# One gathered tile's query: four weight buffers, scores kept in row buffers and searched block by block, steps emitted three at a time

## The chip, the cores and the metric

The kernel runs on one core of a Trainium2 chip. The metric is the time of one execution on the device in microseconds (us), smaller is better. PE is the matrix engine, DVE the vector engine, ACT the scalar engine, POOL the GpSimd engine; SP issues transfers. Each engine works through its own instructions in the order in which they stand.

## What is computed

One layer of a decoder for 1024 prompt tokens and 64 sample tokens: an input projection, two token mixers (retention and a recurrent one), an output projection, then a mixture of experts with product keys, then a gated embedding. The part that matters here is the expert layer:

```python
q = (xb @ wq).reshape(PEER_BLOCK, PEER_HEADS, 2, PEER_DKEY // 2)
s = jnp.einsum('phcd,hcnd->phcn', q, keys)          # 8 heads x 2 halves, 128 keys each
sv, si = lax.top_k(s, 16)
cand = sv[:, :, 0, :, None] + sv[:, :, 1, None, :]
cv, ci = lax.top_k(cand.reshape(...), 16)
e = take(si[:, :, 0], ci // 16) * 128 + take(si[:, :, 1], ci % 16)
gsm = softmax(cv)
hval = einsum('pd,phkd->phk', xb, u_tab[e])         # 128 rows of u_tab per token
y = einsum('phk,phkd->pd', gelu(hval) * gsm, v_tab[e])
```

## The kernel before

The 1088 tokens are nine tiles: 0 to 7 of 128 tokens, tile 8 of 64. Tiles 4 to 7 (`G2`) go through the experts densely: every expert is multiplied with every token and weighted. Tiles 0, 1, 8 (`E0`) and 2, 3 (`G1`) are **gathered**: for each of a token's 128 chosen experts, POOL issues one indirect transfer that brings a row of 1024 numbers for each of 128 tokens into a row buffer (`grow<-in_pu`, later `grow<-in_pv`, line 1144), and DVE multiplies or accumulates it (lines 1158 and 1172). That is 576 + 576 = 1152 transfers. `grow` runs through a ring of row buffers, so POOL issues as DVE frees them.

The program goes through these stages, read off the profile's time table: first projection and mixer (0 to 360 us); the projection of tiles 4 to 8 (`group_a` on `A2`, 360 to about 583 us: first the 40 steps of `a_ret`, with `pret` as the result and `rope`, `gsig`, `retd` behind it, then `a_rw` with `prw`, `rb`, `fdst`); the other mixers with the output rows of each tile (`group_b`, to about 1700); the last rows and the dense tiles' query (to 2060); the hidden layer of the dense tiles with their gates (to 2560); the second half of the dense experts in two parts (to 3577); and the end, `ple`, the gated embedding and final norm for tiles 0, 1, 8, 4 to 7, 2, 3 in this order.

The gathered work is written as one generator, `early`. It emits tile 0's query (`early_query`), then tile 0's gathers with the queries of tiles 1 and 8 threaded in, then the gathers of tiles 1 and 8. During the projection of `A2` each projection step is followed by `IE` steps of `early`; in the mixers by one each, up to 150. What is left comes after the dense query. The emitted order isn't the final one: the program is put through a list scheduler with a timeline model, which moves instructions along each engine, so an emitted place acts as a priority.

`early_query` takes a tile's normed rows (`exn`), turns them (`exT`), and for each of 16 blocks `hc` loads 512 KB of query weights (`ewq`) and 64 KB of keys (`ekT`), makes the query (`epq`, `eqT`) and its 128 scores (`es`). Before, the scores of two blocks are staged in a buffer with tag `sv` or `si` and stored to memory (`sd`); at the end two loads of eight blocks each bring them back, and `topk` searches them with `pick` (five DVE operations a block: two maxima of eight, two index searches, one replacement; lines 1043 to 1047). The tile's results are called `sv` and `si`, and take the buffers with those two tags. Then `topk` sums candidates (`ce`, with `sf` for the indices), searches the sums (`cv`, `ci`), finds the expert numbers with eight `eq` on POOL and eight `ef` on DVE, and writes `eid`; the gathers need `eid`.

Row buffers of the pool `early`, 4 KB a partition each: `V` twice, `W`, `xy`, `Wq` four times, `xT`. Tile 0's query takes its weights through the two `V`; the reloaded scores lie in `W` and a `Wq`. The gathers run through `V`, `V`, `W`, `xy`, and the tile's rows for the products (`gx`) come through `xy`.

Of the kernel before, what the change touches and what calls it, by code (L numbers as in the profile page):

```python
# [8 lines left out]
F32 = mybir.dt.float32  # L9
# [3 lines left out]
U32 = mybir.dt.uint32  # L13
# [168 lines left out]
E0 = [0, 1, 8]  # L182
# [8 lines left out]
IB = 2  # L191
PGT = "a"
SPL = "gv"
IE = 2
IA = 2
G2 = [4, 5, 6, 7]
RSTART = 2
# [2 lines left out]
QB = 4  # L200
# [17 lines left out]
class K:  # L218
# [431 lines left out]
    def first_mix(self, es):  # L650
# [3 lines left out]
        return self.mixers(self.cw, A0[0])  # L654

    def group_b(self, tiles, early):

        done = []
        self.b2 = 2
        with ExitStack() as e:  # L660
# [12 lines left out]
            for i, t in enumerate(tiles + [None]):  # L673
                cur, nxt = nxt, self.mixers(rp, t) if t is not None else None
                if i >= 2:
                    done.append(tiles[i - 2])
                live = nxt is not None
                while live or cur is not None:
                    if cur is not None:
                        if next(cur, "end") == "end":  # L680
                            cur = None
                    if i >= RSTART:
                        for _ in range(RRATE):
                            if next(rows, "end") == "end" and done:
                                rows = self.c_rows(self.co, done.pop(0))
                    if live:
                        live = next(nxt, "end") != "chain"
                    for _ in range(ERATE if E0[1] in self.rowed else 0):
                        if steps < EB:
                            steps += 1  # L690
                            next(early, None)
# [497 lines left out]
    def early_query(self, wp, t, wtag, wbufs, stags):  # L1189

        nc, I = self.nc, self.I
        n = SIZE[t]
        xn = wp.tile([128, D], F32, name="exn", tag=wtag, bufs=wbufs)
        nc.sync.dma_start(xn[:n], self.xd[t][:n])
        xT = wp.tile([128, 8, 128], F32, name="exT", tag="xT")
        for k in range(2):
            p = self.ps("etr", "a").rearrange("p (a b) -> p a b", a=4)
            for j in range(4):
                d = 4 * k + j
                nc.tensor.transpose(p[:, j, :n], xn[:n, d * 128:d * 128 + 128], self.c("ident")[:n, :n])  # L1200
            nc.scalar.activation(xT[:, 4 * k:4 * k + 4, :n], p[:, :, :n], AF.Copy)
            yield
        for hc in range(16):
            kT = wp.tile([128, 128], F32, name="ekT", tag=("cv", "ci")[hc % 2])
            nc.sync.dma_start(kT, I['keysT'][:, hc])
            w = wp.tile([128, 8, 128], F32, name="ewq", tag=wtag, bufs=wbufs)
            nc.sync.dma_start(w, I['wq'][hc])
            if hc % 2 == 0:
                st = wp.tile([128, 2, 128], F32, name="es", tag=("sv", "si")[hc // 2 % 2])
            p = self.ps("epq", "a")  # L1210
            for k in range(8):
                nc.tensor.matmul(p[:, :n], w[:, k], xT[:, k, :n], start=k == 0, stop=k == 7)
            qT = wp.tile([128, 128], F32, name="eqT", tag=("cf", "ef")[hc % 2])
            nc.scalar.activation(qT[:, :n], p[:, :n], AF.Copy)
            nc.tensor.matmul(p[:n, 128:256], qT[:, :n], kT, start=True, stop=True)
            nc.scalar.activation(st[:n, hc % 2], p[:n, 128:256], AF.Copy)
            if hc % 2:
                nc.scalar.dma_start(self.sd[t][:n, hc - 1:hc + 1], st[:n])
            yield
        s = []  # L1220
        for j in range(2):
            s.append(wp.tile([128, 8, 128], F32, name="es", tag=stags[j], bufs=QB if stags[j] == "Wq" else 1))
            nc.sync.dma_start(s[j][:n], self.sd[t][:n, 8 * j:8 * j + 8])
        yield
        ce = wp.tile([128, 2, 8, 50], F32, name="ce", tag="Wq", bufs=QB)
        yield from self.topk(wp, t, [s[j // 8][:, j % 8] for j in range(16)], dict(eq=dict(tag="xT")), (ce[:, 0], ce[:, 1]))

    def early(self, wp):

        rows = ("V", "V", "W", "xy")  # L1230
        yield from self.early_query(wp, E0[0], "V", 2, ("W", "Wq"))
        g = self.gather(wp, E0[0], rows, acc=self.acc)
        for t in E0[1:]:
            while t not in self.rowed:
                next(g, None)
                yield
            for _ in self.early_query(wp, t, "Wq", QB, ("Wq", "xT")):
                next(g, None)
                yield
        yield from g  # L1240
        for t in E0[1:]:
            yield from self.gather(wp, t, rows + ("xT",) * (t == E0[-1]), acc=self.acc)
# [201 lines left out]
    def build(self):  # L1444
# [3 lines left out]
        with self.es:  # L1448
# [28 lines left out]
            for _ in a:  # L1477
                for _ in range(IE):
                    next(early, None)
# [100 lines left out]
```

## Time and profile before

| | us |
|---|---|
| Median of 3 runs | 3758.44 |
| The three runs | 3747.60, 3758.44, 3776.36 |
| The profiled execution | 3747.65 |
| Its span, first to last instruction | 3745.9 |
| PE busy | 3294.1 |
| DVE busy | 2856.0 |
| POOL busy | 2336.2 |
| ACT busy | 1217.6 |

The profile is of one execution; what follows is read from it. A row of the timeline gives start, length, engine, line, operation, output and input, and in brackets how long the engine had been idle and for whom. A row of the table by stretch gives for each engine its busy time and number of instructions, then the granted PE clock (1.00 is full), the share of the transfer engines in use, and GB/s.

### The profile page before, as it was taken

The numbers are of one execution on the slowest core, as the hardware profiler recorded it, in microseconds if no ns is written. First come the engines' busy times: TensorE is split into PE (matmuls) and PEld (weight loads), VectorE is DVE, ScalarE is ACT, GpSimd is POOL, SyncE is SP. The second block draws the span as 40 slices with busy tenths as digits, with TensorE's granted clock in tenths as the row PEclk, the third lists the DMA queues.
The fourth block names the chain that finished last, engine by engine and source line by source line (L and its number), as shares of the span: only waits on it lengthen the run. The fifth ranks groups of instructions, "written<-read, shape, count | busy, mean of one in ns | idle before, by whom it ended". The sixth has DMA issues, their size and how long they took to land. (4 is left out here: it accounts for less than half of the span.)

```text
span 3745.9 us, 52394 instructions
## 1 busy us (share of the span) xinstructions
PE 3294.1 (88%) x17749; PEld 2742.5 (73%) x17749; DVE 2856.0 (76%) x5655; ACT 1217.6 (33%) x2260; POOL 2336.2 (62%) x2068
## 2 busy tenths in 40 slices
PE   7799995868869978884899999998999999989979
PEld 7698994644747866673787888887888877767757
DVE  4454388878797698886897998875777787888885
ACT  4232220111202111211222788793333333333322
POOL 5364176455364555554558877867888888888751
PEclk9799995667968566876999999999999999999989
DMA  7266578889778877888769888899999999999982
GB/s 254 81 216 212 187 244 289 276 286 311 258 249 313 311 268 253 285 273 320 254 216 317 298 311 320 332 340 334 337 347 342 328 354 371 374 370 368 339 279 89
DMA packets 425286, 1077.84 MB, mean 288 GB/s; under 512 B 46459, under 2 KB 144505, under 8 KB 420346
## 3 DMA queue, kind: packets, MB, share of 16 engines
q0 software_dynamic: 165888, 604.05, 45.5%
q1 hardware_dynamic: 203102, 378.60, 30.6%
q10 hardware_dynamic: 56028, 91.84, 6.6%
q8 instruction: 141, 2.31, 0.2%
q14 instruction: 127, 1.04, 0.1%
HBM read 982.51 MB, written 91.75 MB: 287 GB/s over the span
## 5 line engine op out<-in xcount | busy, mean ns | idle before, releaser
L1144 POOL DMA_INDIRECT grow<-in_pv,eid x576 | 567.4, 985 | 464.1 <-DVE gacc L1172 289.0
L1144 POOL DMA_INDIRECT grow<-in_pu,eid x576 | 558.1, 969 | 405.6 <-DVE grow L1158 228.0
L1172 DVE SCALAR_TENSOR_TENSOR gacc<-grow,ac,gacc 128x1024 f32<-128x1024 f32 x571 | 731.8, 1282 | 87.0 <-DMA grow<-in_pv,eid 80.3
L1158 DVE SCALAR_TENSOR_TENSOR grow<-grow,gacc 128x1024 f32<-128x1024 f32 x576 | 691.6, 1213 | 131.0 <-DMA grow<-in_pu,eid 124.1
L332 PE MATMUL ph<-cx,uh 128*128 128x512 f32 x1024 | 406.3, 397 | 17.5 <-DVE al L305 9.8
L1318 PE MATMUL py<-ah,vh 128*128 128x512 f32 x1024 | 403.3, 394 | 19.7 <-ACT vh L303 19.7
L333 PE MATMUL ph<-cx,uh 128*128 128x512 f32 x1024 | 404.9, 395 | 0.0
L1319 PE MATMUL py<-al,vh 128*128 128x512 f32 x1024 | 402.4, 393 | 2.6 <-DVE al L305 2.6
L307 POOL TENSOR_TENSOR vl<-vraw,vh 128x640 fp32r<-128x640 f32 (+1 forms) x224 | 326.2, 1460 | 34.9 <-ACT vh L303 17.5
L307 POOL TENSOR_TENSOR ul<-uraw,uh 128x1024 fp32r<-128x1024 f32 x128 | 307.7, 2404 | 64.5 <-issue 26.8
L1321 PE MATMUL py<-ah,vl 128*128 128x512 f32 x1024 | 275.9, 397 | 11.4 <-POOL vl L307 11.1
L335 PE MATMUL ph<-cx,ul 128*128 128x512 f32 x1024 | 263.2, 395 | 2.9 <-POOL ul L307 2.9
L303 ACT ACTIVATE vh<-vraw 128x640 fp32r<-128x640 f32 (+1 forms) x224 | 154.9, 692 | 301.8 <-DMA vraw<-in_pvd 105.6
L1318 PEld LDWEIGHTS py<-ah,vh 128*128 128x128 f32 x1024 | 193.5, 189 | 68.5 <-ACT vh L303 27.0
L332 PEld LDWEIGHTS ph<-cx,uh 128*128 128x128 f32 x1024 | 194.5, 190 | 58.0 <-DVE al L305 10.2
L1321 PEld LDWEIGHTS py<-ah,vl 128*128 128x128 f32 x1024 | 191.5, 189 | 61.7 <-POOL vl L307 20.7
L1319 PEld LDWEIGHTS py<-al,vh 128*128 128x128 f32 x1024 | 193.8, 189 | 44.4 <-DVE al L305 3.9
L1325 DVE TENSOR_TENSOR yT<-yT,py 128x512 f32<-128x512 f32 x216 | 147.7, 684 | 98.2 <-PE py L1321 86.8
L333 PEld LDWEIGHTS ph<-cx,uh 128*128 128x128 f32 x1024 | 194.4, 190 | 38.4
L335 PEld LDWEIGHTS ph<-cx,ul 128*128 128x128 f32 x1024 | 191.1, 189 | 42.0 <-POOL ul L307 4.0
L307 POOL TENSOR_TENSOR wl<-wraw,wh 128x1024 fp32r<-128x1024 f32 x45 | 114.7, 2550 | 114.2 <-ACT wh L303 96.3
L303 ACT ACTIVATE uh<-uraw 128x1024 fp32r<-128x1024 f32 x128 | 135.2, 1056 | 151.8 <-DMA uraw<-in_puT 91.4
(401 smaller groups left out, 7352.7 us busy)
## 6 DMA issues: line engine op xcount, KB each, us to landing
uraw<-in_puT SPq DMA_DIRECT2D x128, 512.0 KB
vraw<-in_pvd SPq DMA_DIRECT2D x128, 320.0 KB
cw<-in_w_out SPq DMA_DIRECT2D x128, 256.0 KB
wd<-wst ACTq DMA_DIRECT2D x28, 1024.0 KB
wt<-wd SPq DMA_DIRECT2D x64, 448.0 KB
wraw<-in_w_ret SPq DMA_DIRECT2D x48, 512.0 KB
ewq<-in_wq SPq DMA_DIRECT2D x48, 512.0 KB
vraw<-in_pvd SPq DMA_DIRECT2D x96, 256.0 KB
```

The lines of the kernel that those rows point to most:

```text
L303: nc.scalar.activation(hi, src, AF.Copy)
L307: nc.gpsimd.tensor_tensor(lo, src, hi.bitcast(F32), op=OP.subtract)
L332: mm(out, lh(k), rh(k), start=first and k == 0, stop=False)
L333: mm(out, *((ll(k), rh(k)) if right else (lh(k), rl(k))), start=False, stop=False)
L335: mm(out, *((lh(k), rl(k)) if right else (ll(k), rh(k))), start=False, stop=last and k == nk - 1)
L1144: nc.gpsimd.indirect_dma_start(out=g, out_offset=None, in_=src, in_offset=bass.IndirectOffsetOnAxis(ap=self.eid[t][:, j:j + 1], axis=0))
L1158: nc.vector.scalar_tensor_tensor(g[:, c], g[:, c], 1.0, x[:, c], op0=OP.mult, op1=OP.mult, accum_out=hv[:, i, j:j + 1])
L1172: nc.vector.scalar_tensor_tensor(y[:, c], g[:, c], ac[:, j:j + 1], y[:, c], op0=OP.mult, op1=OP.add)
L1318: nc.tensor.matmul(p, vh[:, b, :], ah, start=b == 0, stop=False)
L1319: nc.tensor.matmul(p, vh[:, b, :], al, start=False, stop=False)
L1321: nc.tensor.matmul(p, vl[:, b, :], ah, start=False, stop=b == nb - 1)
L1325: nc.vector.tensor_tensor(yT[:, d, :], yT[:, d, :], p, op=OP.add)
```

## The change

For tile 0 alone (`here` in the code; the other two queries stay as they were): the rows and the weights go through the four `Wq` buffers; the scores stay on the chip, blocks 0 to 7 in `W` and 8 to 15 in `xy`; each block is searched right after its scores are there, in `early_query`; `topk` then starts at the candidate sums. The eight stores to `sd` and the two loads go. `IE` goes from 2 to 3. Tile 0's query now has 16 steps fewer, since `topk` no longer has the search as steps.

```diff
-IE = 2
+IE = 3
@@ early_query
+        here = not isinstance(stags[0], str)
+        if here:
+            s = [wp.tile([128, 8, 128], F32, name="es", tag=g) for g, in stags]
+            self.found = {t: (wp.tile([128, 16, 16], F32, name="sv"), wp.tile([128, 16, 16], U32, name="si"))}
         for hc in range(16):
...
-            if hc % 2 == 0:
+            if here:
+                st = s[hc // 8][:, hc // 2 * 2 % 8:hc // 2 * 2 % 8 + 2]
+            elif hc % 2 == 0:
                 st = wp.tile([128, 2, 128], F32, name="es", tag=("sv", "si")[hc // 2 % 2])
...
             nc.scalar.activation(st[:n, hc % 2], p[:n, 128:256], AF.Copy)
-            if hc % 2:
+            if here:
+                self.pick(self.found[t], hc, st[:, hc % 2], n)
+            elif hc % 2:
                 nc.scalar.dma_start(self.sd[t][:n, hc - 1:hc + 1], st[:n])
             yield
-        s = []
-        for j in range(2):
+        if not here:
+            s = []
+        for j in range(0 if here else 2):
             s.append(...)
             nc.sync.dma_start(s[j][:n], self.sd[t][:n, 8 * j:8 * j + 8])
         yield
         ce = wp.tile([128, 2, 8, 50], F32, name="ce", tag="Wq", bufs=QB)
-        yield from self.topk(wp, t, [s[j // 8][:, j % 8] for j in range(16)], dict(eq=dict(tag="xT")), (ce[:, 0], ce[:, 1]))
+        yield from self.topk(wp, t, None if here else [s[j // 8][:, j % 8] for j in range(16)], dict(eq=dict(tag="xT")), (ce[:, 0], ce[:, 1]))
@@ early
-        yield from self.early_query(wp, E0[0], "V", 2, ("W", "Wq"))
+        yield from self.early_query(wp, E0[0], "Wq", QB, (("W",), ("xy",)))
```

Three places in the order of instructions show what moves. On DVE, the search of tile 0 during the projection of `A2`. Before, it starts behind the last product with `rope` and a `wl` (the low part of a split projection weight), eight blocks at once:

```order
L397 TENSOR_TENSOR ropeA<-pret,rope 64x256
L398 TENSOR_TENSOR ropeB<-pret,rope 64x256
L305 TENSOR_TENSOR wl<-wraw,wh 128x1024
L1043 MAX sv<-es 128x8 x8
L1044 MAX_INDEX si<-sv,es 128x8 x6
L1045 MATCH_REPLACE es<-sv,es 128x128
```

With the change:

```order
L397 TENSOR_TENSOR ropeA<-pret,rope 128x256
L398 TENSOR_TENSOR ropeB<-pret,rope 128x256
L1043 MAX sv<-es 128x8
L1044 MAX_INDEX si<-sv,es 128x8
L397 TENSOR_TENSOR ropeA<-pret,rope 128x256
L398 TENSOR_TENSOR ropeB<-pret,rope 128x256
L1045 MATCH_REPLACE es<-sv,es 128x128
L1046 MAX sv<-es 128x8
```

The search now stands between the products of the projection, from the first block on.

On POOL, the stretch from the candidate sums of tile 0's expert numbers (`ce`) to its first gathers. Before:

```order
L1083 TENSOR_TENSOR ce<-sf 128x8x8
L307 TENSOR_TENSOR wl<-wraw,wh 128x1024
L1099 TENSOR_TENSOR eq<-ce,cf 128x800 x5
L307 TENSOR_TENSOR wl<-wraw,wh 128x1024
L1099 TENSOR_TENSOR eq<-ce,cf 128x800
L557 TENSOR_TENSOR fdst<-rb 128x512
L562 TENSOR_TENSOR fdst<-rs 128x64
L1099 TENSOR_TENSOR eq<-ce,cf 128x800 x2
L307 TENSOR_TENSOR wl<-wraw,wh 128x1024
L557 TENSOR_TENSOR fdst<-rb 128x512
L562 TENSOR_TENSOR fdst<-rs 128x64
L1144 DMA grow<-in_pu,eid_64 128x1024 x4
```

With the change:

```order
L1083 TENSOR_TENSOR ce<-sf 128x8x8
L307 TENSOR_TENSOR wl<-wraw,wh 128x1024
L1099 TENSOR_TENSOR eq<-ce,cf 128x800 x4
L307 TENSOR_TENSOR wl<-wraw,wh 128x1024
L1099 TENSOR_TENSOR eq<-ce,cf 128x800 x4
L307 TENSOR_TENSOR wl<-wraw,wh 128x1024
L1144 DMA grow<-in_pu,eid_64 128x1024 x4
L557 TENSOR_TENSOR fdst<-rb 128x512
L562 TENSOR_TENSOR fdst<-rs 128x64
L1144 DMA grow<-in_pu,eid_64 128x1024
```

The first gathers moved from behind the second `fdst` (the mixed projection rows of `a_rw`) to ahead of the first. The last `wl` ahead of them is now the one that stood between the fifth and the sixth `eq` before. Counted along POOL, 35 gathers stood ahead of the last `fdst` before, and 39 now; 536 and 541 ahead of the first split of the hidden layer (`ul`), 1120 and 1134 ahead of the last `vl` of the dense experts.

The third place is POOL at the end, in `ple` (`nrs` and `frs` are small scale factors of the norms), before:

```order
L1144 DMA grow<-in_pv,eid_68 128x1024 x11
L297 TENSOR_SCALAR nrs<-nssq 128x1
L298 TENSOR_TENSOR nrs<-nrs,halves 128x1
L1144 DMA grow<-in_pv,eid_68 128x1024 x5
L297 TENSOR_SCALAR nrs<-nssq 128x1
L298 TENSOR_TENSOR nrs<-nrs,halves 128x1
L1144 DMA grow<-in_pv,eid_68 128x1024 x6
L297 TENSOR_SCALAR nrs<-nssq 64x1
L298 TENSOR_TENSOR nrs<-nrs,halves 64x1
L1144 DMA grow<-in_pv,eid_68 128x1024
L297 TENSOR_SCALAR frs<-fssq 128x1
```

With the change:

```order
L1144 DMA grow<-in_pv,eid_68 128x1024 x10
L297 TENSOR_SCALAR nrs<-nssq 128x1
L298 TENSOR_TENSOR nrs<-nrs,halves 128x1
L1144 DMA grow<-in_pv,eid_68 128x1024 x5
L297 TENSOR_SCALAR nrs<-nssq 128x1
L298 TENSOR_TENSOR nrs<-nrs,halves 128x1
L1144 DMA grow<-in_pv,eid_68 128x1024 x3
L297 TENSOR_SCALAR nrs<-nssq 64x1
L298 TENSOR_TENSOR nrs<-nrs,halves 64x1
L297 TENSOR_SCALAR frs<-fssq 128x1
L298 TENSOR_TENSOR frs<-frs,halves 128x1
```

Before, ten more gathers stand behind the third `nrs`; now none does.

## Prediction

> **What bounds the kernel.** I read the page's busy times first, then its costliest groups, then the busy times by stretch, because one average covers stages with different limits.
>
> ```profile
> PE 3294.1 (88%) x17749; PEld 2742.5 (73%) x17749; DVE 2856.0 (76%) x5655; ACT 1217.6 (33%) x2260; POOL 2336.2 (62%) x2068
> ...
> L1144 POOL DMA_INDIRECT grow<-in_pv,eid x576 | 567.4, 985 | 464.1 <-DVE gacc L1172 289.0
> L1144 POOL DMA_INDIRECT grow<-in_pu,eid x576 | 558.1, 969 | 405.6 <-DVE grow L1158 228.0
> L1172 DVE SCALAR_TENSOR_TENSOR gacc<-grow,ac,gacc 128x1024 f32<-128x1024 f32 x571 | 731.8, 1282 | 87.0 <-DMA grow<-in_pv,eid 80.3
> ```
>
> ```profile
> 360.00:500.00 140.00, 132.58 (x1092) 131.72 (x1091) 63.41 (x264) 34.23 (x78) 43.34 (x43) 0.98 0.58 187
> 500.00:620.00 120.00, 91.02 (x628) 88.07 (x626) 101.65 (x201) 24.25 (x59) 85.43 (x89) 0.83 0.91 307
> 620.00:1000.00 380.00, 297.01 (x1792) 220.30 (x1791) 307.93 (x503) 53.66 (x122) 189.39 (x183) 0.73 0.87 290
> 1000.00:1400.00 400.00, 325.70 (x1596) 258.48 (x1594) 326.79 (x828) 58.22 (x136) 204.88 (x213) 0.68 0.80 277
> ...
> 2060.00:2560.00 500.00, 485.57 (x2608) 414.66 (x2607) 427.72 (x800) 390.17 (x813) 378.83 (x299) 0.99 0.89 323
> 2560.00:3050.00 490.00, 480.24 (x2105) 396.16 (x2104) 362.32 (x496) 152.43 (x226) 406.81 (x331) 0.99 0.95 336
> 3050.00:3577.00 527.00, 491.31 (x2076) 389.45 (x2074) 431.69 (x684) 194.53 (x320) 427.79 (x356) 0.99 1.01 362
> ```
>
> The columns are stretch, length, then busy PE, weight load, DVE, ACT and POOL, then the granted PE clock, the share of the transfer engines and GB/s. Where the change is (360 to 500), PE is busy 132.6 of 140 us: PE sets that stage. In the mixers (620 to 1400) no engine is full: PE 80%, DVE 81%, at a granted clock of 0.68 to 0.73; they hand work to each other. From 2060 to 3050 PE is busy 97 to 98%. So a gather that comes earlier pays only if some stage behind it has less to do for that, and the question is which.
>
> **What the change removes from tile 0's query.** The chain from the last score to the first gather:
>
> ```profile
> 434.60 1.65 DVE L1043 MAX8 sv<-es 128x8 f32<-128x128 f32 x8 [11.43 <-DMA sd<-es]
> 446.20 0.28 DVE L1043 MAX8 sv<-es 128x8 f32<-128x128 f32 x1
> 461.50 0.28 DVE L1047 FIND_INDEX8 si<-sv,es 128x8 uint32<-128x128 f32 x1
> ```
> ```profile
> 439.05 0.28 ACT L1216 ACTIVATE es<-epq 128x128 f32<-128x128 f32 x1 [2.45 <-PE epq L1215]
> 439.36 0.33 ACTq L1218 DMA_DIRECT2D sd<-es  x1
> ```
> ```profile
> 409.36 0.33 SPq L1223 DMA_DIRECT2D es<-sd  x1
> ...
> 441.25 0.33 SPq L1223 DMA_DIRECT2D es<-sd  x1
> ```
> ```profile
> 486.54 2.45 POOL L307 TENSOR_TENSOR wl<-wraw,wh 128x1024 fp32r<-128x1024 f32 x1
> ...
> 501.66 1.44 POOL L1144 DMA_INDIRECT grow<-in_pu,eid  x1 [0.19 <-issue]
> ```
>
> The scores of blocks 0 to 7 were asked back at 409.4, yet their search starts at 434.6, and what ends DVE's wait is a *store* of scores: `sv` takes the buffer from which scores were still being stored. For blocks 8 to 15 the trip out and back lasts from 439.36 to 446.20, 6.8 us. The search ends at 461.78. With the change neither wait is there. The last score doesn't come earlier, though: PE is full here, and in the order it stands behind 2116 projection matmuls where it stood behind 2111, which at 0.12 us each from start to start is 0.6 us later, about 439.9. Behind it two blocks are left to search, ten operations at 0.28 us or less, so the search ends near 442.7: **19 us earlier**.
>
> From the search's end to the first gather it took 501.66 - 461.78 = 39.9 us. Nothing in that chain gets shorter, which would put the first gather at 482.6. But on POOL it now stands behind the `wl` that ran at 486.54 to 488.99, and that one follows the projection's pace. I take 489.2: the first gather comes **12.5 us earlier** (19 at most).
>
> ```profile
> 500.00:620.00 120.00, 55.45 (x53) 0.83 0.91 307
> ```
>
> That is POOL in the gathers alone: 53 in 120 us, one per 2.26 us, so 12.5 us are 5.5 gathers. The order says the same: 39 ahead of the last `fdst` instead of 35.
>
> **What each stage then does.** *360 to 500.* PE idles 7.4 us in all. The waits of PE there have one large row:
>
> ```profile
> PE pret L332 <- DVE retd L408: 4.7, 1, 4.7
> ```
>
> `retd` waited behind the late search on DVE. That search is now spread between the `rope` products. The gain lies between 0 and 7.4; I take 3. The spread adds a wait as well: a search that waits on DVE for its score holds up the `ropeA` products behind it, and PE waits for those to free its result. DVE is busy less than half of the stage, so I put this at 0; one hold like the row above would be +4.7.
>
> *Extra weight buffers.* They bring loads forward, three in a row on SP ahead of a `rope` load. What could be late is the projection's weight:
>
> ```profile
> 371.10 0.33 SPq L375 DMA_DIRECT2D wraw<-in_w_ret  x1
> ```
> ```profile
> 389.01 2.01 ACT L303 ACTIVATE wh<-wraw 128x1024 fp32r<-128x1024 f32 x2 [0.28 <-PE pret L333]
> ```
>
> It is asked for 18 us before ACT uses it, and ACT then waits for PE. Two loads of 512 KB more at the stage's 187 GB/s are 5.6 us: hidden, price 0. The eight stores of 128 KB and two loads of 512 KB that go are 2.1 MB, 11 us of transfer at that rate, in a stage with 42% of the transfer engines free: also 0. `gx` is new behind the search, since it needs `xy`: on SP two `wraw` of the next part stand behind it. Before, the first of those was issued at 447; the search ends before that, so 0 as well.
>
> *The mixers, to 1700.* On POOL, between the last `fdst` (35 gathers ahead of it before, 39 now) and the seventh `crs` of a full tile (456, now 459) stand 420 gathers instead of 421; along DVE it is 419 products instead of 422 between the same places. I take -2, between 0 and -7 (three fewer at 2.26 us each).
>
> *2060 to 3577.* 536 against 541 gathers stand ahead of the first `ul`, 1120 against 1134 ahead of the last `vl`: nine more inside these stages. At 1.28 us of DVE each that is 11.5 us of DVE where PE is 93 to 98% busy and DVE idles 14 to 26%. PE covers them: I take +2; without cover +11.5.
>
> *The end, from 3577.* Fourteen gathers fewer, 18 us of DVE less. But:
>
> ```profile
> 3598.00:3739.00 141.00, 137.07 (x636) 109.26 (x636) 105.14 (x139) 41.27 (x76) 42.03 (x53) 0.98 0.47 153
> ```
> ```profile
> 3664.36 1.27 DVE L1172 SCALAR_TENSOR_TENSOR gacc<-grow,ac,gacc 128x1024 f32<-128x1024 f32 x1
> ```
> ```profile
> 3685.49 4.37 DMA ph<-hd
> ```
>
> PE idles 3.9 us of 141. The last gather was used at 3665.6, and the last tile, which needs it, loads its rows only at 3685.5, when a buffer is free. So at most -3.9; I take -1.
>
> **Sum.** -3 - 2 + 2 - 1 = -4 us, with all good ends -7.4 - 7 - 3.9 = -18, with all bad ends +4.7 + 11.5 = +16. The profiled execution took 3747.65; that gives 3744, from 3729 to 3764. The median of the runs lies 10.8 above the profiled execution, so on it I forecast **3754**, from 3740 to 3774; the runs before spread by 29 us themselves. Within 1% (38 us) a change of this kernel can't be told from none.
>
> **Rivals.** *The gathers are the bound* (chance 0.14). For: 1152 of them run almost without a gap from 501.66 to 3665.6, one per 2.75 us, and POOL waits most for DVE to free a row. Then an earlier start comes off the end: 12.5 to 19 us, so 3739 to 3746. Against: the 20 us of slack at 3665.6, and that the order moves the gathers against the other work by different numbers at different places.
>
> *The clock falls out otherwise, to the good* (0.13) or, on the other side, *to the bad* (0.11). What the mixers take hangs on the granted clock:
>
> ```profile
> 1140.00:1200.00 60.00, 55.96 (x375) 45.03 (x375) 43.44 (x73) 15.04 (x33) 24.71 (x27) 0.94 0.86 304
> 1200.00:1320.00 120.00, 117.05 (x474) 99.93 (x475) 81.39 (x152) 15.37 (x43) 59.74 (x61) 0.50 0.90 316
> ```
>
> For 120 us PE is 98% busy at half clock, right behind 60 us at 0.94. The change shifts how the queries of tiles 1 and 8 lie among the mixers. If that stretch ran at full clock, PE would need 59 us, DVE's 81 would bound it, and 33 to 39 us would go (120 less 81 to 87): 3715 to 3721. The other way, if the 60 us ahead of it fell to half clock, its 56 us of PE would become about 105: +45 us, 3799. It decides as soon as PE has over 80% to do in a stretch, so that a slower clock can't hide in its idle time.
>
> The Trainium skill, "TensorE: Matmul & The Clock Gate", Part 1, says that PE gets its full clock after one busy window of about 3.4 us and loses it after an idle one. By that rule the stretch at 1200 would be at full clock and the denser query could only help; the row, 0.50 at 98% busy, contradicts it, so it changes neither chance.
>
> *POOL is late at the end of `a_rw`* (0.06, slower). Four gathers now stand ahead of the first `fdst`, and PE ends that stage on a wait:
>
> ```profile
> PE psh L570 <- DVE shl L564: 11.3, 1, 11.3
> ```
>
> Four to five gathers at 1.05 us on POOL could lengthen it by 5 us, and by twice that if the mixers' start slips too: 3763 to 3769. It decides if `rb` has no free buffer while POOL issues.
>
> *The change does nothing of what it says*: the scheduler, not `IE`, places the steps, and PE's part of the query is no denser at its end. That is in the sum already; if the first gather doesn't move at all, the time is 3758.
>
> **How the numbers follow.** Forecast (with the last rival) 0.56, gathers as bound 0.14, clock good 0.13, clock bad 0.11, POOL 0.06. Faster by over 1% is below 3721: most of the good clock and some scatter of the runs, 0.12. Slower by over 1% is above 3796: most of the bad clock, 0.08. Within 1%: 0.80. For 8 in 10 the range takes the forecast's ends, the gather and POOL cases, the good clock's upper half and the approach to the bad one's: 3717 to 3790.
>
> **What would show it.** The first `grow` near 489 and the search's end near 443 (the first two steps); the PE wait for `retd` gone; first `fdst` no later than about 493; the last `gacc` some 30 us ahead of the last `ph<-hd` instead of 20; PE still 97% busy from 3598 on. If the first gather comes by 480, or the mixers' end moves by more than 10 us without a change of clock, the sum is wrong in its middle; if the clock column between 620 and 1700 differs by over 0.04, the clock rival decided.

## The result, and the profile after

| | before | changed |
|---|---|---|
| first comparison: median (runs) | 3764.09 (20) | 3744.39 (20) |
| ratio, 95% interval | | 0.994 (0.9923 to 0.9956) |
| second comparison: median (runs) | 3766.20 (25) | 3732.62 (8) |
| ratio, 95% interval | | 0.993 (0.9905 to 0.9955) |
| span of the first profile | 3745.9 | 3732.4 |
| span of the second profile | 3760.1 | 3717.9 |

By the ratios the changed kernel is 0.6 to 0.7% faster, 22 to 26 us, and neither interval holds 1; the medians lie 20 and 34 us apart. The forecast was 4 us less. The profiles of one kernel differ by 14 us, so stages are compared below on two profiles each. Three of these four executions are at the fast end of their kernel's runs (3747.65, 3734.53 and 3719.95), so stages that differ by a few us say little.

The page of the changed kernel. The busy times barely differ from before, and the gathers cost the same:

```profile
PE 3291.0 (88%) x17749; PEld 2732.8 (73%) x17749; DVE 2851.4 (76%) x5655; ACT 1219.3 (33%) x2260; POOL 2335.5 (63%) x2068
...
L1144 POOL DMA_INDIRECT grow<-in_pv,eid x576 | 562.6, 977 | 431.2 <-DVE gacc L1172 254.6
L1144 POOL DMA_INDIRECT grow<-in_pu,eid x576 | 562.8, 977 | 422.0 <-DVE grow L1158 242.0
L1172 DVE SCALAR_TENSOR_TENSOR gacc<-grow,ac,gacc 128x1024 f32<-128x1024 f32 x571 | 731.8, 1282 | 86.8 <-DMA grow<-in_pv,eid 74.3
```

The table by stretch of the changed kernel, in the stretches shown of before:

```profile
360.00:500.00 140.00, 139.71 (x1168) 139.24 (x1167) 75.67 (x288) 36.80 (x83) 57.99 (x56) 1.00 0.62 207
500.00:620.00 120.00, 79.89 (x534) 75.88 (x532) 101.87 (x198) 20.89 (x54) 83.72 (x85) 0.78 0.90 301
620.00:1000.00 380.00, 306.71 (x1821) 229.37 (x1822) 310.36 (x494) 54.85 (x122) 186.12 (x183) 0.71 0.86 291
1000.00:1400.00 400.00, 327.39 (x1618) 258.50 (x1615) 324.63 (x846) 57.42 (x136) 207.23 (x211) 0.69 0.79 271
```

In the first row PE has 0.3 us left of 140 where it had 7.4, the clock is 1.00 where it was 0.98, and 1168 matmuls are done where 1092 were. The timeline of tile 0's query in the changed kernel:

```profile
436.69 0.45 ACT L1222 ACTIVATE es<-epq 128x128 f32<-128x128 f32 x2 [0.40 <-PE epq L1221]
...
439.85 0.28 DVE L1047 FIND_INDEX8 si<-sv,es 128x8 uint32<-128x128 f32 x1
```
```profile
469.91 1.54 POOL L1099 TENSOR_TENSOR eq<-ce,cf 128x800 f32<-128x800 f32 x1 [1.10 <-DVE ef L1101]
471.41 3.39 POOL L307 TENSOR_TENSOR wl<-wraw,wh 128x1024 fp32r<-128x1024 f32 x1
475.39 1.21 POOL L1144 DMA_INDIRECT grow<-in_pu,eid  x1 [0.58 <-DVE eid L1125]
```

The search ends at 440.1 (before 461.8), 3 us behind the last score, and the first gather is issued at 475.4 (before 501.7; in the second profiles 477.4 and 505.4). To see where the time went, I cut both kernels at the same instructions instead of at the same times; a length runs from the start of one to the start of the next:

| from ... to | before, twice | changed, twice | means |
|---|---|---|---|
| start, first `crs` | 352.5, 355.5 | 350.3, 352.5 | -2.6 |
| projection of `A2`: to the last `fdst` | 229.4, 230.4 | 220.6, 219.3 | -10.0 |
| mixers: to the last `crs` | 1210.8, 1213.9 | 1198.3, 1185.0 | -20.7 |
| last rows, query: to the first `ul` | 146.0, 144.9 | 148.0, 149.3 | +3.2 |
| hidden layer: to the first `vl` | 635.4, 636.2 | 633.5, 637.5 | -0.3 |
| fused half: to the last `ul` | 452.4, 452.8 | 451.2, 451.2 | -1.4 |
| stored half: to the last `vl` | 541.9, 547.4 | 557.6, 550.9 | +9.6 |
| end: to the last `fin` | 173.8, 175.1 | 168.1, 167.6 | -6.6 |

So the mixers gain most, the projection 10 us, and the stored half gives 10 us back. The first row is scatter: nothing differs there in the emitted code. At the end the last gather, tile 3's, is used at 3611.4. The rows of tile 2 are loaded at 3671.1, and tile 3's stored sum (`yd`) is read back at 3676.8, 64 us behind its last gather. PE is as full as before (141 us from the same place in `ple`):

```profile
3611.41 1.28 DVE L1172 SCALAR_TENSOR_TENSOR gacc<-grow,ac,gacc 128x1024 f32<-128x1024 f32 x1
```
```profile
3671.05 4.50 DMA ph<-hd
```
```profile
3676.82 0.32 SPq L1421 DMA_DIRECT2D py<-yd  x1
```
```profile
3584.50:3725.50 141.00, 136.49 (x636) 109.19 (x636) 90.72 (x125) 42.29 (x77) 24.56 (x41) 0.98 0.35 111
```

### The profile page after: what moved, and what is told of

It is laid out like the page before. It is cut to its first block, busy times and chain, and to the rows that moved or that the text cites. A ratio compares the mean times of both kernels' runs of the same rounds, so it can differ in the third digit from the quotient of the medians.

```text
span 3732.4 us, 52377 instructions
## 1 busy us (share of the span) xinstructions
PE 3291.0 (88%) x17749; PEld 2732.8 (73%) x17749; DVE 2851.4 (76%) x5655; ACT 1219.3 (33%) x2260; POOL 2335.5 (63%) x2068
## 5 line engine op out<-in xcount | busy, mean ns | idle before, releaser
L1327 PEld LDWEIGHTS py<-ah,vh 128*128 128x128 f32 x1024 | 194.9, 190 | 79.9 <-ACT vh L303 35.3
L1273 ACT ACTIVATE oh<-oh,it 128x128 f32<-128x128 f32 x512 | 159.9, 393 | 36.5 <-DVE oh L1271 27.5
```

Of the source, the lines that this page charges most:

```text
L1273: nc.scalar.activation(oh[:, 0, j], oh[:, 0, j], AF.Copy, scale=it[:, s + b + j:s + b + j + 1])
L1327: nc.tensor.matmul(p, vh[:, b, :], ah, start=b == 0, stop=False)
```

## The experiments

Theory 1: the gathers start earlier, and the kernel ends earlier for it. Theory 2: the denser emission is the gain. Theory 3: the list scheduler makes another order, and the order decides the length of the later stages. Theory 4: the clock granted in the mixers carries their length. Theories G, D and P are three prices of a gather behind 2060 us.

### One part of the change at a time

**The query alone**, from the changed kernel:

```diff
-IE = 3
+IE = 2
```

> The change of the query alone: scores on the chip, four weight buffers, IE back at 2. In the order the first gather stands ahead of the second fdst of the last projection, 38 gathers stand ahead of its last fdst (35 before, 39 with the whole change) and 490 ahead of the last crs (489 and 494). Theory 1 (the earlier start of the gathers is the gain): first grow near 476, last fdst about 11 us earlier than before, ratio to before 0.993 to 0.996. Theory 2 (the denser emission is the gain): first grow early too, but the ratio 0.998 to 1.002. Theory 3 (each order falls out by itself in the mixers, between the last fdst and the last crs): ratio anywhere from 0.990 to 1.006, and the mixers' length off the changed kernel's 1214 us by 10 or more either way.

Measured: 0.9977 (0.9956 to 0.9999), first `grow` 486.2, projection 222.0, mixers 1223.9 us.

**IE alone**, from the kernel before:

```diff
-IE = 2
+IE = 3
```

> The kernel before with IE at 3 alone: scores still stored and read back, weights through the two V. In the order the first gather stands behind the third fdst, 33 gathers ahead of the last fdst and 483 ahead of the last crs. Theory 1 (start of the gathers): first grow 500 or later, last fdst within 3 us of 582, ratio 0.998 to 1.003. Theory 2 (denser emission): ratio 0.993 to 0.996. Theory 3 (each order falls out by itself): 0.990 to 1.006, with the mixers off 1227 us by 10 or more.

Measured: 0.9998 (0.9979 to 1.0017), first `grow` 509.3, projection 230.8, mixers 1187.1 (in the fastest of its 12 runs).

**Four weight buffers, scores through memory**, from the kernel before:

```diff
-IE = 2
+IE = 3
-        yield from self.early_query(wp, E0[0], "V", 2, ("W", "Wq"))
+        yield from self.early_query(wp, E0[0], "Wq", QB, ("W", "xy"))
```

> Four weight buffers and IE at 3, but tile 0's scores go to memory and back as before (read back into W and xy). First gather behind the third fdst as with IE 3 alone; 33 gathers ahead of the last fdst, 492 ahead of the last crs. Theory 1: the weight buffers give nothing, ratio 0.998 to 1.003, first grow 500 or later. If instead the four buffers (loads further ahead) carry the gain: 0.993 to 0.996. Theory 3: 0.990 to 1.006, no relation to the start.

Measured: 0.9964 (0.9944 to 0.9984), first `grow` 510.5, projection 232.4, mixers 1205.2.

**Scores on the chip, two weight buffers**, from the changed kernel:

```diff
-        yield from self.early_query(wp, E0[0], "Wq", QB, (("W",), ("xy",)))
+        yield from self.early_query(wp, E0[0], "V", 2, (("W",), ("xy",)))
```

> The whole change but with tile 0's weights through the two V as before. The order starts the gathers at the same place as the whole change (39 ahead of the last fdst), but 482 stand ahead of the last crs instead of 494. Theory 1: first grow near 476, ratio 0.993 to 0.996, the same as the whole change within 0.002. If the four buffers are needed: 0.998 to 1.002. Theory 3: off the whole change by more than 0.003 though the gathers start at the same time.

Measured: 0.9974 (0.9944 to 1.0004), first `grow` 481.1, projection 227.9, mixers 1212.4.

What follows. Theory 1 isn't borne out: two kernels with an early start gain 0.23 and 0.26%, and the one with the latest start of all gains 0.36%. Their intervals overlap, so a small share of it is not excluded. Theory 2 falls as a cause by itself, since IE alone gives nothing; that it helps only together with the query is not excluded. The parts hardly add up either: 0.9977 and 0.9998, each uncertain by 0.002, make 0.9975, and the whole is 0.993 to 0.994. But the projection is settled. PE's largest waits from 350 to 500 us, first of IE alone, then of the query alone, then with two buffers:

```profile
PE pret L332 <- DVE retd L408: 6.0, 1, 6.0
```
```profile
PE pret L332 <- DVE retd L408: 0.8, 1, 0.8
```
```profile
PE epq L1218 <- DMA ewq<-in_wq: 1.6, 1, 1.6
PE pret L332 <- DVE retd L408: 1.5, 2, 1.0
```

Every kernel that stores the scores waits 4.7 to 6.6 us for `retd`, which stands on DVE behind the search of eight blocks; in every one with the scores on the chip that wait is 1.5 us or less. With two buffers PE waits for weights as well, and the projection gains only 2 us of the 10. And the wait costs more than itself. The kernel before, around it:

```profile
453.62 1.70 PE L335 MATMUL pret<-wl,x 128*128 128x256 f32 x12 [1.70 <-DVE wl L305]
459.99 0.58 PE L332 MATMUL pret<-wh,x 128*128 128x256 f32 x1 [4.67 <-DVE retd L408]
```
```profile
450.00:459.40 9.40, 3.62 (x29) 3.22 (x27) 9.40 (x61) 0.77 (x2) 0.00 (x0) 0.99 0.18 61
459.40:466.20 6.80, 6.21 (x29) 6.21 (x30) 6.80 (x56) 0.77 (x2) 1.97 (x6) 0.51 0.18 60
```

PE works 3.6 of 9.4 us, and the next 6.8 us are granted at half clock. Half of the 6.2 us that PE works there is lost: 3 us, on top of 7 us of idle time from 360 to 500. Together that is the 10. The same 6.8 us stand in the clock record of all four profiles whose scores go through memory, and in none of the ten others.

### The same kernels again, and other orders from the same start

**The kernel before, again**, with a profile:

> The kernel before, profiled a second time, to see how far one kernel's stages differ from execution to execution. Theory 3 (the order of the instructions fixes each stage): last fdst, last crs, first ul and last vl within 3 us of the first profile's distances from each other (229, 1211, 146, 635, 994 us). Theory 4 (the granted clock in the mixers scatters from execution to execution and carries their length): the mixers between 1185 and 1225 us, with the half-clock time in them moving the same way, about 2 us of it per us of length, and the other stages as in the first profile.

Measured: 3761.85 us; projection 230.4, mixers 1213.9, the rest in the table above.

**The changed kernel, again:**

> The changed kernel, profiled a second time and timed beside the other variants. Ratio 0.992 to 0.996 as in the first comparison. Theory 3: last fdst near 571 and mixers 1198 us again, within 3 us. Theory 4: last fdst near 571 again (that part is the search's and runs at full clock), mixers 1185 to 1225 us with the half-clock time.

Measured: 0.993 (0.9905 to 0.9955); projection 219.3, mixers 1185.0.

**16, 48 and 8 empty steps behind tile 0's query**, from the changed kernel (8 steps were timed later, against runs of the kernel before of their own, with a median of 3761.51):

```diff
         yield from self.early_query(wp, E0[0], "Wq", QB, (("W",), ("xy",)))
+        for _ in range(16):
+            yield
```

> The changed kernel with 16 empty steps between tile 0's query and its gathers, so that the gathers are emitted as late as if the search still were 16 steps. In the order the first gather stays where it is (40 gathers ahead of the last fdst instead of 39), 489 ahead of the last crs instead of 494. Theory 1 (start of the gathers): ratio as the changed kernel's within 0.001, 0.993 to 0.996. Theory 3 (order in the mixers and after): the five gathers fewer ahead of the last crs make it 0.996 to 0.999. Theory 4: 0.993 to 0.997, scattering with the clock.

Measured: 0.9959 (0.9929 to 0.999), projection 222.6, mixers 1212.7.

> The same with 48 empty steps: 39 gathers ahead of the last fdst, 496 ahead of the last crs, 545 ahead of the first ul. Theory 1: as the changed kernel, 0.993 to 0.996. Theory 3: as the changed kernel or up to 0.002 below, since two to four gathers more are done by then. Theory 4: 0.993 to 0.997.

Measured: 0.9954 (0.9934 to 0.9974), projection 217.4, mixers 1219.8.

> The changed kernel with 8 empty steps behind tile 0's query: the same start of the gathers (40 ahead of the last fdst), but the list scheduler orders the rest otherwise: 376 gathers ahead of the fifth crs (381), 485 ahead of the last (494), 1116 ahead of the last vl (1134), 36 behind it instead of 18. Theory 1 (start): 0.992 to 0.996. Theory 3 (the order that comes out decides): the nine gathers fewer shorten the mixers or not, but 18 more at the end cost 5 to 10 us there as in the other kernels with 30 or more left, ratio 0.995 to 0.999. Theory 4: 0.992 to 0.998.

Measured: 0.9899 (0.9868 to 0.993), a median of 3727.92 us, the lowest of all kernels that leave nothing out. Its profile spans 11 us more than that: projection 218.3, mixers 1226.1, stored half 539.0.

What follows. An empty step issues nothing; it only shifts what the scheduler compares. With the same instructions and the first gather at 476.7 to 478.5 in all three, the ratios run from 0.9899 to 0.9959. So by the ratios the order that happens to come out is worth as much as the whole change. This rests on 6 to 12 runs each: the intervals of 8 and 48 steps just miss each other, and those of 8 and 16 just touch. Theory 3 can't say which order is good, though: by its counts of gathers 8 steps were to be no better than 16, and they were the best. Nor is the order all: two executions of the changed kernel have mixers of 1198 and 1185 us, a scatter that theory 4 expected and theory 3 did not.

### The price of a late gather, and of a denser mix

**40 gathers less at the end**, from the changed kernel (in `gather`; the slices of `hv`, `ac` and `gsm` follow):

```diff
+        m = n - 20 if t == 8 else n
-        for j in range(n):
+        for j in range(m):
```

> The changed kernel without the last 20 of tile 8's 64 gathers from each table: 40 transfers and 40 DVE products fewer, all of them after 2000 us (that tile's result is then incomplete; nothing else is left out). Up to the first ul the order is that of the changed kernel. Theory G (the gathers are the bound, 2.7 us each): about 100 us below the changed kernel, ratio to before 0.966 to 0.970. Theory D (their DVE time is the price, 1.28 us each): 51 us below, 0.979 to 0.982. Theory P (PE covers them after 2060 us): at most the 10 us that the stored half of the dense experts took more with the change, and 6 us of the end, 0.989 to 0.994. In the mixers: theory 3 (order fixes the length) 1185 to 1200 us again, theory 4 (the clock scatters) 1185 to 1225 us.

Measured: 0.9883 (0.986 to 0.9906), 3721.23 us. Against the changed kernel's 0.993 to 0.994 that is 0.005 to 0.006, some 18 to 21 us, half a us per gather; the interval just touches that of the second comparison. In the profile the mixers took 1202.0, the hidden layer 626.2 (9 us less; the other kernels lie between 629.5 and 652.1), the stored half 558.1 and the end 163.3 (5 us less). G (100 us) and D (51 us) fall; P is nearest, and lies just above the result. Even the half us is no sure price: the kernel with 8 empty steps, which has all its gathers, lies at 0.9899, so another order behind the first `ul` could give as much.

**Two gather steps per mixer step**, from the changed kernel:

```diff
-ERATE = 1
+ERATE = 2
```

> The changed kernel with two steps of the gathered work per step of the mixers (ERATE at 2): 388 gathers ahead of the fifth crs of the mixers instead of 381, 505 ahead of the last crs instead of 494, 1144 ahead of the last vl instead of 1134, all done before ple. A try at a better version. Theory 1 or G (earlier gathers are worth their lead): ratio to before 0.985 to 0.992. Theory 3 (a gather costs about 2 us in the mixers where it is placed, and nothing behind them): the mixers 11 to 25 us longer than the changed kernel's, ratio 0.996 to 1.001. Theory 4: 0.992 to 0.998, with the clock in the mixers.

Measured: 1.0053 (1.0037 to 1.0069): slower than before, and than any theory said. More gathers stand ahead of each later stage, and the mixers take 1249.6 us, 51 to 65 more than the changed kernel's, with 11 gathers more. Its first gather is issued at 477.4, so an early start alone doesn't make a kernel faster.

**IE at 4**, from the changed kernel:

```diff
-IE = 3
+IE = 4
```

> The changed kernel with IE at 4 instead of 3: first gather ahead of the second fdst, 37 gathers ahead of the last fdst, 379 ahead of the fifth crs, 486 ahead of the last, 1121 ahead of the last vl. Theory 1: first grow near 485, last fdst near 575, ratio 0.993 to 0.997. Theory 2 (the denser, the better): 0.990 to 0.993. Theory 3: between 0.992 and 1.000 with the order that comes out, the projection (first crs to last fdst) 217 to 223 us as in every kernel with scores on the chip and four weight buffers.

Measured: 0.9933 (0.9907 to 0.9959), first `grow` 487.1, projection 222.8, mixers 1196.2. Denser is not shown to be better: the interval is that of IE at 3.

### What the mixers' length consists of

In each kernel the same 5053 matmuls lie between the last `fdst` and the last `crs`. The table by stretch, cut there: before twice, the changed kernel twice, 40 gathers less (whose order is the changed kernel's up to the first `ul`), IE alone, 8 empty steps, and ERATE at 2:

```profile
582.00:1793.00 1211.00, 940.45 (x5053) 731.18 (x5053) 971.21 (x1831) 183.27 (x391) 624.05 (x621) 0.71 0.83 284
```
```profile
586.00:1800.00 1214.00, 942.72 (x5053) 732.30 (x5053) 969.14 (x1831) 183.53 (x391) 622.41 (x621) 0.70 0.84 283
```
```profile
571.00:1769.00 1198.00, 932.93 (x5053) 721.94 (x5053) 973.04 (x1828) 183.46 (x391) 625.14 (x620) 0.71 0.84 287
```
```profile
572.00:1757.00 1185.00, 924.23 (x5053) 713.96 (x5053) 973.27 (x1829) 183.53 (x391) 624.26 (x622) 0.71 0.86 290
```
```profile
569.00:1771.00 1202.00, 934.54 (x5053) 722.11 (x5053) 974.30 (x1829) 182.95 (x391) 624.17 (x622) 0.71 0.84 286
```
```profile
586.00:1773.00 1187.00, 902.31 (x5053) 691.31 (x5053) 964.85 (x1829) 183.53 (x391) 621.71 (x616) 0.72 0.85 287
```
```profile
571.00:1797.00 1226.00, 939.80 (x5053) 733.09 (x5053) 961.49 (x1816) 183.88 (x391) 610.16 (x612) 0.70 0.82 276
```
```profile
569.00:1819.00 1250.00, 949.77 (x5053) 739.74 (x5053) 988.02 (x1840) 183.71 (x391) 634.39 (x634) 0.69 0.83 281
```

DVE's work is the same to 3% in all, and so are the matmuls, yet PE is busy from 902 to 950 us with them. Read off the clock record of all 14 profiles, the time at half clock in the mixers lies between 658 and 768 us, and PE's busy time goes with it, 0.41 us for each us (correlation 0.88; without ERATE at 2, 0.48 and 0.89). That is about the half that PE loses in a us at half clock while it has work. PE's idle time, 259 to 300 us, does not go with it (correlation 0.20), and it spreads the length about as much as the busy time does. The length, the sum of both, goes with the half clock by 0.50 us for each us (0.86; 0.41 and 0.78). The Trainium skill says the same of the loss in "TensorE: Matmul & The Clock Gate", Terms: the penalty is the throttled time times the share of the clock that is missing, here a half. The stored half moves with it too: from 539.0 us with 6.8 us at half clock (8 empty steps) to 558.1 with 34.1 (40 gathers less), 0.67 us per us, correlation 0.90. Half of 27 us is 14 of these 19, so waits must come with it.

From before to changed, PE's busy time for the 5053 matmuls falls from 941.6 (mean of two) to 930.6 (of three), 11 us, and its idle time from 270.9 to 264.4, 6.5 us: together the 17 us by which the three profiles with the changed order are shorter. Nearly all of it lies in one place. Cut into eight parts of equally many matmuls (of the 632 in the fourth, 602 are the same before and after), the fourth part takes 172.9 and 174.0 us before, and 155.2, 154.1 and 156.1 in the changed order; the other seven together differ by 1 us. Before and changed:

```profile
1001.40:1174.30 172.90, 122.54 (x636) 90.48 (x634) 152.79 (x357) 24.25 (x51) 92.52 (x93) 0.75 0.75 259
```
```profile
997.70:1152.90 155.20, 117.25 (x634) 84.94 (x633) 135.91 (x349) 24.05 (x51) 84.29 (x83) 0.79 0.77 263
```

DVE is busy 88% of both, and has 17 us less to do in the second, with 45 products of gathered rows in place of 52; half clock falls from 85 and 96 us to between 65 and 72. The order has moved DVE's work out of a part where DVE is nearly full. That is argued from the rows, not tested apart from the clock.

That the length goes with the clock is shown; which comes first is not. A length of waits lowers the clock (above, at 459 us), and three executions of the changed order differ by 20 us in half-clock time and 17 in length. What in an order makes the clock fall I didn't find. One stretch shows that idle time is not all of it. Tile 8's query, in the changed kernel and in IE alone:

```profile
1194.00:1290.00 96.00, 94.12 (x382) 80.51 (x379) 62.92 (x113) 12.66 (x37) 46.74 (x46) 0.50 0.84 291
```
```profile
1194.00:1294.00 100.00, 89.53 (x560) 77.31 (x558) 70.26 (x128) 16.84 (x46) 52.14 (x53) 0.78 0.90 319
```

PE is 98% busy at 0.50 in the one; in the other it is 90% busy at 0.78 and gets 560 matmuls done instead of 382. The order doesn't fix it either. Tile 8's query again, in the first and in the second execution of the changed kernel:

```profile
1170.00:1284.00 114.00, 109.49 (x506) 95.98 (x506) 74.29 (x135) 15.72 (x48) 57.58 (x58) 0.56 0.85 295
```
```profile
1158.00:1268.00 110.00, 99.27 (x508) 86.54 (x506) 72.88 (x130) 15.67 (x48) 56.37 (x56) 0.63 0.86 298
```

## Why the prediction was right, and where not

The time lay inside the range and moved the way that was forecast, but by 22 to 26 us where the sum had 4. That it stayed in the range is in part luck: the mixers brought 21 us where 2 were forecast, the stored half took 10 back, and the base of three runs, 3758.44, lay 6 us below the median of 20. The signs that I had named say so too: the first gather came ahead of 480, and the mixers' end moved by 23 us while the clock column changed by no more than 0.03 (0.71, 0.69 and 0.78 where it was 0.73, 0.68 and 0.75), so the sum was wrong in its middle. And a change of under 1% could be told from none after all, with 20 runs of each. Step by step:

- *The search ends 19 us earlier:* 21.7. The last score came at 437.1 instead of 439.9, since the kernel was 2 us earlier from the start. Right.
- *First gather 12.5 us earlier:* 26. The failed step is "that one follows the projection's pace", said of the `wl` at 486.54. Its row has no bracket: POOL had not been idle ahead of it, so it stood behind late `eq` in POOL's queue, not behind the projection. With the `eq` early, it ran at 471.41, directly behind one. "Nothing in that chain gets shorter" failed too, which is why even the 19 us at most were passed: from the search's end to the first gather it took 35.3 us instead of 39.9. The first `eq` came 3 us sooner behind the search's end, and the two pairs of `fdst`, 1.3 us each, now stand behind the gathers.
- *360 to 500, -3, at most -7.4:* -10. The mechanism was right (PE's wait for `retd`), and the bound was too small: it counted the idle time and left out that PE comes back at half clock, 3 us more. The +4.7 for products held up behind the spread search didn't come: PE idles 0.3 us.
- *Extra buffers and gx, 0:* right for gx. For the buffers the rank was wrong: they are no free extras. With two, PE waits 1.6 us for weights, 1.5 for `retd` and, in `a_rw`, 2.5 for `rs`, and the projection takes 227.9 instead of about 220 (one profile).
- *The mixers, -2, at most -7:* -17 to -21. Mis-sized: I priced the mixers by the number of gathers (420 against 421) and so held the rest as fixed. PE's time for the same matmuls moved by 11 us and its idle time by 6.5, most of it in the part from 1001 to 1174 us, where seven products fewer fall.
- *2060 to 3577, +2, at most +11.5:* +8. The size was inside the bounds, the reason was not. The price of nine more gathers isn't it: seven of them fall into the hidden layer, which is no longer than before; the stored half has 203 and 204, and takes 558 us again in the kernel with 40 fewer, which has 202 there. Its length went with the half clock instead; what causes either isn't shown.
- *The end, -1, at most -3.9:* -6.6. The bound was taken from 3598 on, and there PE is as full as before (136.5 of 141 us). Some 4.6 us of the 6.6 lie ahead of that, between the last `vl` and the first `njunk` on DVE (28.9 and 29.5 us before, 25.0 and 24.1 now), where the last dense rows hand over to `ple`. With 40 gathers fewer, and none left by then, that stretch takes 18.0 us. The row at 3685.49 was misread besides: it loads tile 2's rows, and the last gathers are tile 3's, whose sum was read back at 3691.2.

The rivals. *The gathers are the bound* is refuted: 40 fewer at the end bring half a us each, not 2.7, and 64 us lie between the last gather and its reader, not the 30 that I named. *POOL late at the end of `a_rw`* did not come: the first `fdst` ran at 480.7, and PE's wait for `shl` is 11.5 us where it was 11.3. (Its 3763 to 3769 were counted from the time before, not from the forecast.) *The clock* goes with more than half of the mixers' part (11 of 17 us), at about the price that I used (half of the time at half clock), but I had put it as one stretch that flips, at 1200 us, and as a chance apart. It fell out better in the part ahead of that one, from 85 and 96 us of half clock to between 65 and 72, while DVE's work there fell too. My sign for it, 0.04 in the clock column, was too coarse: 0.71 stands in that column for 933 and for 924 us of PE. *The change does nothing of what it says* is half true: IE at 3 alone does nothing (0.9998), the query does.

What is shown: scores on the chip with four buffers shorten the projection, by the wait and the half clock behind it; it takes 217.1 to 222.8 us in the nine profiles that have both, and 229.4 and 230.4 before. What is not: that the other 12 to 16 us belong to the change. Three kernels with the same instructions and the same start lie between 0.9899 and 0.9959, a spread as large as the change. The fastest of them can't be told from the changed kernel by the intervals (0.9868 to 0.993 against 0.9905 to 0.9955).

## What to carry to other kernels

A wait of the matrix engine is to be priced with the clock that follows it: here 7 us of idle time cost 10. A row without a bracket in the timeline says that the engine was busy up to it, so it can move when the queue ahead of it moves. And a stage is to be looked at in parts: the mixers had about as many gathers as before, and became shorter in the one part in which seven fewer fell. And where a scheduler orders the program, an edit that issues nothing (8 empty steps) belongs beside every small gain: here three such edits lie 0.6% apart, so a single variant's 0.6% says little on its cause.

## What the runs showed of the hardware

The same 5053 matmuls took PE from 902 to 950 us, most of it with the time at half clock (correlation 0.88), and two executions of one order differed by 9 us in it. I had expected a stage's PE time to be fixed by its instructions. Half clock was granted for 96 us with PE 98% busy, so a full engine was no sign of a full clock here. The Trainium skill, "TensorE: Matmul & The Clock Gate", Part 1, lets the full clock return after about 3.4 us of sustained work. This stretch doesn't show it, while the 6.8 us at half clock behind the idle stretch at 450 agree with it.
